# A two-layer trunk on one core: the first MLP's first half in four parts of K, and another order of instructions

## The chip, the cores and the metric

The program runs on one core of one Trainium2 chip. The metric is the device time of one execution in microseconds (us). A core has TensorE (PE, matrix products, with its weight loads shown apart as PEld), VectorE (DVE), ScalarE (ACT), GpSimd (POOL) and SyncE (SP), which in this kernel issues nearly all DMA transfers. Each engine runs its own instructions in the order in which the program lists them, and semaphores hold an instruction back until its inputs are there and its output's buffer is free. So the time depends on two things: how much each engine has to do, and in which order each engine's list puts it.

## The reference

The computation is a decoder trunk of two layers on 256 tokens of width 2048, in float32. Each layer has a mixer and an MLP, and each of the four is preceded by a modulated RMS norm and followed by a gated residual:

```python
def ada_modulate(x, c, w, b):
    mod = jax.nn.silu(c) @ w + b
    shift, scale, gate = jnp.split(mod, 3, axis=-1)
    h = rms_norm(x) * (1.0 + scale[:, None, :]) + shift[:, None, :]
    return h, gate[:, None, :]

def sq_relu_mlp(h, w1, w2):
    return jnp.square(jax.nn.relu(h @ w1)) @ w2

for layer in range(DEPTH):                      # DEPTH = 2
    h, gate = ada_modulate(x, c, ada_w[layer, 0], ada_b[layer, 0])
    y = mlstm_mixer(h, ...) if layer % 2 == 0 else rglru_mixer(h, ...)
    x = x + gate * y
    h, gate = ada_modulate(x, c, ada_w[layer, 1], ada_b[layer, 1])
    x = x + gate * sq_relu_mlp(h, mlp_w1[layer], mlp_w2[layer])
return rms_norm(x) * final_g
```

Layer 0's mixer (mLSTM) has a projection to q, k, v, o and two gates, then eight heads with two chunks of 128 tokens each, then a product with `a_w_out`. Layer 1's mixer (RG-LRU) has a projection, a convolution over time, block-diagonal gates and a scan. The MLPs are 2048 to 8192 to 2048. The four `ada_w` matrices, 2048 x 6144 each, multiply one vector `c`.

## The kernel before

**Numbers.** Everything stays transposed: features on the 128 partitions, the 256 tokens on the free axis. A float32 product is made of products of two rounded halves. `split` (L167) makes a high part `whi` on ACT (L174) and a low part `wlo` on DVE (L175) of each half of a weight tile; `pair` (L179) does so for activations (ACT L187 or L184, DVE L188 or L185). A product takes high times high, high times low and low times high. `mm2` (L198) does it in two matmuls, one of 512 columns (L200, both halves of the activation) and one of 256 (L201), and leaves two sums side by side that `halves` (L256) adds with an ACT copy (L260) and a DVE addition (L261). `mm3` (L192) does it in three matmuls of 256 columns (L194 to L196) into one sum. `mmu` (L215) is the form for activations that are not normed yet: `unnormed` (L319) has the scale and the shift in it, and `scaled` (L247) multiplies the result by the norm later, so that the products need not wait for the norm.

**Weights.** Each weight tile is 128 x 2048, 1 MB, and comes in through SP's queue (L161, `raw`) into one of four buffers. After it is split, its halves stand in four buffers for `whi` and four for `wlo`, two tiles' worth.

**Adaptive weights.** The `ada_w` matrices come as 192 tiles of 128 x 2050 (`adaraw`, L125); each costs one DVE instruction (L127) that multiplies it by `c` and adds up the rows. They are spread over the program: `pace(phase, calls)` reads from the table `PACE` how many of the 192 are to be done by the end of a phase, and each `fill()` in the phase issues its share. `need` issues one at once if it is wanted and not there. Outside the first projection these tiles use the same four buffers as the weight tiles.

**Stages.** The projection of layer 0 runs in five groups of K (`GROUPS`, `group` L487): the sums of a group go to SBUF by ACT (L537), and the next group puts them back into PSUM by ACT (L526) ahead of its products. Then come the gates, and the eight heads: `scores` (`sp`, `kp`, `E`, `qw`), `state` (`cp`, `Cn`), `head` (`num`, `den`, `hsq`) and `meansq` (`hss`). Eight weight blocks of the o projection (`ogate` L703, the accumulators from `mm_2710` on) are placed between the steps of the heads by the table `OB`. `normed` makes `zhi` and `zlo`, and the product with `a_w_out` follows: four blocks together from `awoa` (`mm_3675` to `mm_3678`), then twelve from `awo`, each ending in `residual` (L332), which adds to `xall` and squares for the norm. Then layer 0's MLP: its first 4096 hidden columns come from 32 tiles of `w1a`, in two halves of K (`kh`); the first half leaves sums in `part`, the second adds them (L421, L423). The other half of the hidden columns, the second product, layer 1's mixer (`mix1`, L773) and its MLP follow with `block` (L203).

**Order.** The kernel is written as one sequence; the tile framework reserves buffers, sets semaphores and lists each engine's instructions, in program order unless a priority moves them (L173, L126). PSUM has five banks for the products (`ps`, tiles `mm`) and three for other results (`aux`).

Of the kernel before, what the change touches and what calls it, by code (L numbers as in the profile page):

```python
# [8 lines left out]
F32 = mybir.dt.float32  # L9
F32R = mybir.dt.float32r  # L10
AF = mybir.ActivationFunctionType
# [42 lines left out]

QKV_RATE = (1.6, 0.9, 0.9, 0.9, 1)
AHEAD = 2
PACE = dict(o=51, out0=66, w1a=82, w1b=90, mlp0=162, mix1=169, out1=176, mlp1=192)


@with_exitstack  # L60
def trunk_kernel(ctx, tc, xT_d, par_d, ada_d, wqkv_d, wg_d, wo_d, awoa_d, awo_d, bwi_d, bg_d, bwo_d,
# [77 lines left out]
    def pace(phase, calls):  # L139

        pacing[:] = [max(0.0, (PACE[phase] - len(done)) / calls), 0.0]

# [21 lines left out]
    def weights(src):  # L164
        return split(load(src))
# [81 lines left out]
    def scaled(acc, r, out=None):  # L247

        if out is None:
            out = tmp.tile([P, S], F32, name="hsum", tag="t")  # L250
        V.tensor_tensor(out=out, in0=acc[:, 0:S], in1=r, op=ALU.mult)
        c = tmp.tile([P, 1], F32, name="shc", bufs=4)
        V.tensor_scalar(out=c, in0=acc[:, S:S + 1], scalar1=acc[:, S + 1:UX], scalar2=None, op0=ALU.add)
        return out, c
# [52 lines left out]
    def modulated(i, j, r, direct=False):  # L307
        need(i, 16 + j)
        need(i, j)
        t = tmp.tile([P, S], F32, name="hmod", tag="t")  # L310
        V.scalar_tensor_tensor(out=t, in0=xT[j], scalar=mod[i][:, 16 + j:17 + j], in1=r,  # L311
                               op0=ALU.mult, op1=ALU.mult)
        if not direct:
            return pair(t, bias=mod[i][:, j:j + 1])
        h = act.tile([P, 2, S], F32, name="hdirect", tag="act")[:, 0, :]
        A.activation(h, t, AF.Identity, bias=mod[i][:, j:j + 1])
        return h, pair(h)
# [14 lines left out]
    def residual(i, j, acc, norm, us=None, width=KC):  # L332

        need(i, 32 + j)
        for a in range(0, acc.shape[1], S):
            V.scalar_tensor_tensor(out=xT[j], in0=acc[:, a:a + S], scalar=mod[i][:, 32 + j:33 + j],  # L336
                                   in1=xT[j], op0=ALU.mult, op1=ALU.add)
        if norm is not None:
            norm.add(j)
        if us is not None and j < width:  # L340
            us.append(unnormed(i + 1, j))

    def finish(srcs, hid, norm):
# [30 lines left out]
                (nc.sync if i % 8 else nc.scalar).dma_start(out=out_d[:, i:i + 4, ts], in_=x4)  # L374


    def square_relu(h, c, pool):
        A.activation(h, h, AF.Relu, bias=c)  # L378
        A.activation(h, h, AF.Square)
        return pair(h, "more" if pool else "act", pool)  # L380
# [5 lines left out]
    def mlp_in(l, i, norm, us, more):  # L386
        out, us2 = Norm(), []
        hs = []
        pace("mlp1", 32)
        for q in range(FFQ):  # L390
            hid = []
            if l == 0 and q == 0:
                part = []
                for kh in range(2):
                    pace("w1b" if kh else "w1a", 16)
                    if kh == 1:
                        hs += [modulated(i, j, r) for j in range(KC // 2, KC)]
                    for jp in range(16):
                        w = weights(w1a_d[kh, jp])
                        early = kh == 0 and jp < EARLY  # L400
                        if kh == 0:
                            part.append(act.tile([P, 2, S], F32, name="part", tag="act"))
                        for jj in range(2):
                            acc = ps.tile([P, UX if early else 2 * S], F32, name="mm")
                            for kk in range(8):
                                hi, lo = w[kk // 4]
                                o = (kk % 4) * 256 + jj * P
                                (mmu if early else mm2)(acc, hi[:, o:o + P], lo[:, o:o + P],
                                                        us[kk] if early else hs[kh * 8 + kk], kk == 0, kk == 7)
                            if early:  # L410
                                if jp + jj == 0:
                                    r = norm.rstd_now()
                                _, c = scaled(acc, r, part[jp][:, jj, :])
                                A.activation(part[jp][:, jj, :], part[jp][:, jj, :], AF.Identity, bias=c)
                                if jp + jj == 0:
                                    hs += [modulated(i, j, r) for j in range(KC // 2)]
                            elif kh == 0:
                                halves(acc, part[jp][:, jj, :])
                            else:
                                h = tmp.tile([P, S], F32, name="hsum", tag="t")  # L420
                                V.tensor_tensor(out=h, in0=acc[:, 0:S], in1=part[jp][:, jj, :],  # L421
                                                op=ALU.add)
                                V.tensor_tensor(out=h, in0=acc[:, S:2 * S], in1=h, op=ALU.add)  # L423
                                hid.append(square_relu(h, 0.0, more if len(hid) >= 32 - MLP_BUFS else None))
                        fill()
                pace("mlp0", 96)
            else:
                for j in range(32):
                    if l == 1 and q == 0 and j < MORE_MLP:
                        if j == 0:  # L430
                            accs, r = quad([w1b_d[kg] for kg in range(4)], us, norm)
                        if j == 3:
                            hs += [modulated(i, j, r) for j in range(KC)]
                        t, c = scaled(accs[j] if j < 4 else early_block(w1_d[l, j], us), r)
                        hid.append(square_relu(t, c, None))
                    else:
                        hid.append(square_relu(halves(block([w1_d[l, q * 32 + j]], hs)), 0.0,
                                               more if j >= 32 - MLP_BUFS else None))
                    fill()
            for j in range(KC):  # L440
                last = q == FFQ - 1
                if last and l == 1 and j == KC - 1:
                    finish([w2_d[l, 2 * q, j], w2_d[l, 2 * q + 1, j]], hid, out)
                    break
                acc = block([w2_d[l, 2 * q, j], w2_d[l, 2 * q + 1, j]], hid,
                            mm3 if j == KC - 1 else mm2)
                residual(i, j, acc, out if last else None, us2 if last and l == 0 else None)
                fill(2)
        return out, us2
# [108 lines left out]
    with ExitStack() as mctx:  # L558
# [205 lines left out]
                        kg + kk == 6)  # L764
        for j in range(KC):
            acc = accs[j] if j < 4 else block([awo_d[j]], zs, mm3)
            residual(0, j, acc, norm, us, KC // 2)
            fill()

    norm, us = mlp(0, 1, norm, us)  # L770
# [190 lines left out]
```

## Time and profile before

| quantity | value |
|---|---|
| median of 3 runs | 2244.34 us (2240.72 to 2247.15) |
| the profiled execution's own time | 2244.5 us |
| its span in the profile | 2242.8 us |
| mean granted TensorE clock | 0.989 |
| HBM traffic | 596.93 MB read, 267 GB/s over the span |

The span leaves out 1.7 us around the program. In the views below, "busy" is the time in which an engine's records cover the clock, "idle before, releaser" is time ahead of an instruction in which its engine had nothing to do, put down to what ended it, and PEclk is the clock that TensorE was granted as a share of full speed. A slice of 40 in the page is 56 us long. Matmuls overlap in the records (a row's mean of 280 ns is not its pitch), so a rate is read from how many start in a stretch.

### The profile page before, as it was taken

The page shows a single profiled execution, that of the slowest core. Times are in us where ns is not written, and L with a number is a line of the kernel's source. Part 1 is how long each engine was busy: PE and PEld are TensorE (multiplying, and loading weights), DVE is VectorE, ACT ScalarE, POOL GpSimd, SP SyncE. Part 2 cuts the span into 40 slices and gives each one's busy share as a digit, 9 for nine tenths or more (in the row PEclk, how much of TensorE's full clock was granted, in tenths as well). Part 3 has the DMA queues.
Part 4 walks back from the last instruction along what each step waited for, and adds up shares of the span by engine and source line. Part 5 has one row for each costly group of instructions (what it writes and reads, how often), then busy time and mean ns, then how long its engine had stood idle before and what let it go on. Part 6 is the DMA issues. An engine that isn't in the chain of part 4 may idle for free.

```text
span 2242.8 us, 34191 instructions
## 1 busy us (share of the span) xinstructions
PE 2181.7 (97%) x13606; PEld 1960.5 (87%) x13606; DVE 1722.3 (77%) x2199; ACT 1286.1 (57%) x1997; POOL 90.1 (4%) x70
## 2 busy tenths in 40 slices
PE   7899899899999999999999999999999999999998
PEld 6798799788888889888889999889888889888887
DVE  6777888988898788888889988998875555555554
ACT  6677777345674335665445877756664334665443
POOL 0000010220000000000110000020000000000110
PEclk9999999899999999999999999999999999999999
DMA  8888887897788999998997665776875555555552
GB/s 345 348 325 319 307 300 255 303 337 270 285 284 319 337 322 332 328 334 319 322 335 276 211 229 208 269 276 238 307 284 203 188 188 188 188 188 188 189 188 93
DMA packets 88671, 601.25 MB, mean 268 GB/s; under 512 B 10424, under 2 KB 14648, under 8 KB 16192
## 3 DMA queue, kind: packets, MB, share of 16 engines
q1 hardware_dynamic: 86400, 598.03, 74.3%
q8 instruction: 106, 1.74, 0.3%
q10 hardware_dynamic: 2112, 1.05, 0.2%
q14 instruction: 53, 0.43, 0.1%
HBM read 596.93 MB, written 2.11 MB: 267 GB/s over the span
## 4 chain that ended last, share of the span: by engine, by line
PE 86%; DVE 7%; ACT 3%; issue 2%; DMA 1%; SPq 0%; DVEq 0%; ACTq 0%
PE mm L200 42%; PE mm L201 22%; PE mm L511 8%; DVE wlo L175 3%; PE mm L196 2%; PE mm L195 2%; PE mm L194 2%; DVE adaraw L127 2%; ACT whi L174 1%; PE mm L218 1%; PE mm L217 1%; PE mm L219 1%; DMA adaraw<-in_ada 1%; PE mm L357 0%; DVE hmod L311 0%
## 5 line engine op out<-in xcount | busy, mean ns | idle before, releaser
L200 PE MATMUL mm<-pair,whi 128*128 128x512 f32 x4272 | 1496.3, 394 | 5.0 <-DVE pair L188 3.2
L201 PE MATMUL mm<-pair,wlo 128*128 128x256 f32 x4272 | 1195.9, 280 | 0.8 <-DVE wlo L175 0.8
L175 DVE TENSOR_TENSOR wlo<-raw,whi 128x1024 fp32r<-128x1024 f32 x736 | 900.2, 1233 | 380.1 <-ACT whi L174 375.9
L174 ACT ACTIVATE whi<-raw 128x1024 fp32r<-128x1024 f32 x736 | 771.9, 1057 | 609.7 <-PE mm L200 476.7
L200 PEld LDWEIGHTS mm<-pair,whi 128*128 128x128 f32 x4272 | 802.6, 188 | 190.7 <-DVE pair L188 4.7
L201 PEld LDWEIGHTS mm<-pair,wlo 128*128 128x128 f32 x4272 | 804.7, 188 | 1.7 <-DVE wlo L175 1.1
L127 DVE SCALAR_TENSOR_TENSOR adaraw<-adaraw,cbc 128x2050 f32<-128x2050 f32 x192 | 439.7, 2291 | 50.7 <-DMA adaraw<-in_ada 41.7
L511 PE MATMUL mm<-pair,whi 128*128 128x256 f32 x736 | 136.0, 288 | 10.7 <-ACT pair L187 5.7
L511 PEld LDWEIGHTS mm<-pair,whi 128*128 128x128 f32 x736 | 115.8, 194 | 12.9 <-ACT pair L187 6.3
L194 PE MATMUL mm<-pair,whi 128*128 128x256 f32 x432 | 123.1, 285 | 0.0
L195 PE MATMUL mm<-pair,whi 128*128 128x256 f32 x432 | 122.0, 282 | 0.0
L196 PE MATMUL mm<-pair,wlo 128*128 128x256 f32 x432 | 121.4, 281 | 0.0
L511 PE MATMUL mm<-pair,wlo 128*128 128x256 f32 x368 | 104.0, 288 | 2.9 <-DVE wlo L175 2.9
L336 DVE SCALAR_TENSOR_TENSOR xall<-mm,mod,xall 128x256 f32<-128x256 f32 x170 | 81.0, 480 | 27.0 <-PE mm L201 18.7
L378 ACT ACTIVATE hsum<-hsum 128x256 f32<-128x256 f32 x121 | 49.2, 413 | 81.7 <-DVE hsum L261 71.3
L291 POOL TENSOR_TENSOR nacc<-nacc,nsq 128x256 f32<-128x256 f32 x52 | 75.6, 1453 | 351.0 <-ACT nsq L282 350.7
L196 PE MATMUL mm<-zhi,wlo 128*128 128x256 f32 x256 | 75.8, 296 | 6.6 <-DVE wlo L175 6.6
L194 PEld LDWEIGHTS mm<-pair,whi 128*128 128x128 f32 x432 | 81.9, 190 | 0.4
L194 PE MATMUL mm<-zhi,whi 128*128 128x256 f32 x256 | 74.9, 297 | 7.6 <-ACT zhi L731 5.5
L195 PEld LDWEIGHTS mm<-pair,whi 128*128 128x128 f32 x432 | 81.8, 189 | 0.0
L196 PEld LDWEIGHTS mm<-pair,wlo 128*128 128x128 f32 x432 | 81.8, 189 | 0.0
L511 PE MATMUL mm<-whi,pair 128*128 128x512 f32 x256 | 81.0, 394 | 0.0
(218 smaller groups left out, 2054.7 us busy)
## 6 DMA issues: line engine op xcount, KB each, us to landing
raw<-in_w SPq DMA_DIRECT2D x220, 1024.0 KB, 5.1
adaraw<-in_ada SPq DMA_DIRECT2D x192, 1025.0 KB, 6.6
raw<-in_wqkv SPq DMA_DIRECT2D x40, 1024.0 KB, 8.5
raw<-in_w1a SPq DMA_DIRECT2D x32, 1024.0 KB, 6.2
raw<-in_bwi SPq DMA_DIRECT2D x28, 1024.0 KB, 5.0
raw<-in_bwo SPq DMA_DIRECT2D x16, 1024.0 KB, 5.1
raw<-in_awo SPq DMA_DIRECT2D x12, 1024.0 KB, 5.5
raw<-in_wo SPq DMA_DIRECT2D x8, 1024.0 KB, 6.2
```

Of the source, the lines that this page charges most:

```text
L127: V.scalar_tensor_tensor(out=raw, in0=raw, scalar=1.0, in1=cbc, op0=ALU.mult, op1=ALU.mult, accum_out=mod[i][:, j:j + 1])
L174: A.activation(hi, sl, AF.Copy)
L175: V.tensor_tensor(out=lo, in0=sl, in1=hi.bitcast(F32), op=ALU.subtract)
L194: PE.matmul(out, lhsT=whi, rhs=hi, start=first, stop=False)
L195: PE.matmul(out, lhsT=whi, rhs=lo, start=False, stop=False)
L196: PE.matmul(out, lhsT=wlo, rhs=hi, start=False, stop=last)
L200: PE.matmul(out, lhsT=whi, rhs=p.rearrange("p a t -> p (a t)"), start=first, stop=False)
L201: PE.matmul(out[:, 0:S], lhsT=wlo, rhs=p[:, 0, :], start=False, stop=last)
L291: G.tensor_tensor(out=self.acc, in0=self.acc, in1=sq, op=ALU.add)
L336: V.scalar_tensor_tensor(out=xT[j], in0=acc[:, a:a + S], scalar=mod[i][:, 32 + j:33 + j], in1=xT[j], op0=ALU.mult, op1=ALU.add)
L378: A.activation(h, h, AF.Relu, bias=c)
L511: PE.matmul(out, lhsT=l, rhs=m, start=clear and kk + n == 0, stop=kk == gn - 1 and n == len(ops) - 1, skip_group_check=True)
```

## The change

Three things change. The first half of layer 0's first MLP product runs in four parts of K (`kg`) instead of two, with eight tiles of 512 columns each. Two blocks of 128 columns share a PSUM bank. `go_on` makes three matmuls of 256 columns per product as `mm3` does. From the second part on, ACT copies the sums from `part` back into PSUM ahead of the products; after the first three parts ACT copies them out; after the fourth, ACT applies relu to 512 columns at a time, DVE squares, and `pair` splits. `early_part` does the first two tiles on activations that are not normed yet, four at a time, so `residual` now makes four of these (after blocks 8, 10, 12 and 14) instead of eight (after blocks 0 to 7). The weights are laid out for this on the host.

The table `PACE` now asks for 58 adaptive tiles by the end of the product with `a_w_out` instead of 66, and for 66, 74, 82 and 84 by the ends of the four parts instead of 82 and 90 by the ends of the two halves. What it asks for at the end of the MLP and later is the same.

The tile framework is told to order the instructions by its own simulated time line. That applies to the whole program.

```diff
-PACE = dict(o=51, out0=66, w1a=82, w1b=90, mlp0=162, mix1=169, out1=176, mlp1=192)
+PACE = dict(o=51, out0=58, w1_0=66, w1_1=74, w1_2=82, w1_3=84, mlp0=162, mix1=169, out1=176, mlp1=192)
...
-        if us is not None and j < width:
+        if us is not None and width == 4:
+            if j >= KC // 2 and j % 2 == 0:
+                us.append(unnormed(i + 1, j // 2 - 4))
+        elif us is not None:
             us.append(unnormed(i + 1, j))
...
+    def go_on(out, whi, wlo, p, clear, last):
+        ops = ((whi, p[:, 0, :]), (whi, p[:, 1, :]), (wlo, p[:, 0, :]))
+        for n, (lhsT, rhs) in enumerate(ops):
+            PE.matmul(out, lhsT=lhsT, rhs=rhs, start=clear and n == 0, stop=last and n == 2,
+                      skip_group_check=True)
+
+    def early_part(w, us, norm, part):
+        accs = []
+        for b in range(4):
+            acc = ps.tile([P, UX], F32, name="mm")
+            for kk in range(4):
+                hi, lo = w[kk // 2]
+                o = kk % 2 * 512 + b * P
+                mmu(acc, hi[:, o:o + P], lo[:, o:o + P], us[kk], kk == 0, kk == 3)
+            accs.append(acc)
+        if norm is not None:
+            norm.now = norm.rstd_now()
+            norms[:] = [norm.now]
+        for b, acc in enumerate(accs):
+            t = part[b // 2][:, b % 2, :]
+            _, c = scaled(acc, norms[0], t)
+            A.activation(t, t, AF.Identity, bias=c)
...
+                for kg in range(4):
+                    pace(f"w1_{kg}", 6)
+                    for c in range(8):
+                        if kg == 0 and c == 1:
+                            hs += [modulated(i, j, r) for j in range(4)]
+                        w = weights(w1a_d[kg, c])
...
+                            for b2 in range(2):
+                                acc = ps.tile([P, 2, S], F32, name="mm")
+                                sums = part[2 * c + b2]
+                                if kg > 0:
+                                    A.activation(acc, sums, AF.Copy)
+                                for jj in range(2):
+                                    for kk in range(4):
+                                        hi, lo = w[kk // 2]
+                                        o = kk % 2 * 512 + (2 * b2 + jj) * P
+                                        go_on(acc[:, jj, :], hi[:, o:o + P], lo[:, o:o + P], hs[4 * kg + kk],
+                                              kg + jj + kk == 0, kk == 3)
+                                if kg < 3:
+                                    A.activation(sums, acc, AF.Copy)
+                                    continue
+                                A.activation(sums, acc, AF.Relu)
+                                V.tensor_tensor(out=sums, in0=sums, in1=sums, op=ALU.mult)
+                                for jj in range(2):
+                                    own = len(hid) < 32 - MLP_BUFS
+                                    hid.append(pair(sums[:, jj, :], "act" if own else "more", None if own else more))
+                        if c < 6:
+                            fill()
+                        elif c == 6 and kg < 3:
+                            hs += [modulated(i, j, r) for j in range(4 * kg + 4, 4 * kg + 8)]
...
-            residual(0, j, acc, norm, us, KC // 2)
+            residual(0, j, acc, norm, us, 4)
...
-    with tile.TileContext(nc) as tc:
+    with tile.TileContext(nc, schedule_with_timeline_sim=True) as tc:
```

Three places show how the order moves. The first is PE's list between head 0 and head 1 of the mLSTM, before: the end of head 0 (`den`), the next head's scores (`sp`, `kp`), and the first of the `mm_2908` matmuls, a block of the o projection.

```order
L676 MATMUL den_2866<-E_2780,ones_85 128x128
L677 MATMUL den_2866<-qw_2785,Cn_2794 128x128
L639 MATMUL sp_2882<-qk0_187,qk4_191 128x128 x2
L194 MATMUL mm_2908<-pair_220,whi_2911 128x256
L641 MATMUL kp_2885<-ident_87,qk4_191 128x128
L195 MATMUL mm_2908<-pair_220,whi_2911 128x256
L196 MATMUL mm_2908<-pair_220,wlo_2912 128x256
L194 MATMUL mm_2908<-pair_233,whi_2911 128x256
```

In all, 21 matmuls of `mm_2908` stand between `kp` and `hss` there, and 26 more between `cp` and `num`. The same place in the changed program, from the end of head 0 to head 1's `num`:

```order
L708 MATMUL num_2859<-qw_2785,Cn_2794 128x128
L712 MATMUL den_2866<-qw_2785,Cn_2794 128x128
L674 MATMUL sp_2882<-qk0_187,qk4_191 128x128 x2
L676 MATMUL kp_2885<-ident_87,qk4_191 128x128
L728 MATMUL hss_2899<-hsq_2877,ones_85 128x256
L729 MATMUL hss_2899<-hsq_2877,ones_85 128x256
L696 MATMUL cp_2903<-v0_195,kw_2887 128x256
L697 MATMUL cp_2903<-ones_85,kw_2887 128x128
L706 MATMUL num_2972<-E_2889,v0_195 128x128
L707 MATMUL num_2972<-E_2889,v1_196 128x128
```

The o blocks have moved: seven of the eight now stand ahead of head 0's `cp`, 166 matmuls of them between `kp` and `cp` of head 0, and the last, `mm_3522`, is spread over the steps of heads 1 and 2. Later heads have pieces of `mm_3675` to `mm_3678` between their steps.

The second place is SP's list of DMA issues around the start of the product with `a_w_out`, before (rows of the same kind are counted, as x6):

```order
L161 DMA raw<-in_awoa 128x2048 x2
L634 DMA MB<-rows_d 128x512
L125 DMA adaraw<-in_ada 128x2050 x6
L161 DMA raw<-in_awo 128x2048
L125 DMA adaraw<-in_ada 128x2050 x2
L161 DMA raw<-in_awo 128x2048
L125 DMA adaraw<-in_ada 128x2050 x2
L161 DMA raw<-in_awo 128x2048
L125 DMA adaraw<-in_ada 128x2050 x2
L161 DMA raw<-in_awo 128x2048
```

and after:

```order
L161 DMA raw<-in_awoa 128x2048
L669 DMA MB<-rows_d 128x512
L125 DMA adaraw<-in_ada 128x2050
L669 DMA MB<-rows_d 128x512
L125 DMA adaraw<-in_ada 128x2050
L161 DMA raw<-in_awo 128x2048
L669 DMA MB<-rows_d 128x512
L161 DMA raw<-in_awo 128x2048
L669 DMA MB<-rows_d 128x512 x2
L125 DMA adaraw<-in_ada 128x2050
L161 DMA raw<-in_awo 128x2048 x2
```

Between the last `awoa` tile and the last `awo` tile, 22 adaptive tiles are issued before and 7 after; the others come in the MLP.

The third place is ACT's list at the end of layer 1's mixer, after: `th`, `aa`, `TT` and `gb` belong to the last blocks of the recurrence, and `whi_14723` is the second half of the fourth of the weight tiles (`bwo`) of the product that follows.

```order
L184 ACTIVATE pair_14537<-gb_14114 128x256
L874 ACTIVATE aa_13951<-th_14383,sp4_11954 128x256
L876 ACTIVATE TT_13949<-th_14383,sp2_11932 128x256
L871 ACTIVATE th_14394<-gacc_14387,hbra_11956 128x256
L897 ACT_TABLE_LOAD
L897 ACTIVATE gb_14398<-gb_14398 128x512
L895 ACT_TABLE_LOAD
L895 ACTIVATE TT_13949<-TT_13949 128x512
L174 ACTIVATE whi_14723<-raw_14717 128x1024
```

and before, where the same recurrence ends:

```order
L839 ACTIVATE aa_13563<-th_13995,sp4_11566 128x256
L174 ACTIVATE whi_14226<-raw_14220 128x1024
L841 ACTIVATE TT_13561<-th_13995,sp2_11544 128x256
L855 ACTIVATE gb_14010<-mm_14011 128x256
L855 ACTIVATE gb_14010<-mm_14071 128x256
L860 ACT_TABLE_LOAD
L860 ACTIVATE TT_13561<-TT_13561 128x512
L174 ACTIVATE whi_14278<-raw_14276 128x1024
L862 ACT_TABLE_LOAD
```

Before, weight halves stand between the steps of the recurrence; after, none stands between `pair_14537` and `TT_13949`.

More of the change, by code (lines that the diff above doesn't have):

```diff
@@ L374, in finish @@
                 (nc.sync if i % 8 else nc.scalar).dma_start(out=out_d[:, i:i + 4, ts], in_=x4)
+    def go_on(out, whi, wlo, p, clear, last):
[19 more added lines that the diff above has]
+            A.activation(t, t, AF.Identity, bias=c)
+    norms = []
     def square_relu(h, c, pool):
@@ L393, in mlp_in @@
                 part = []
[L394 to L425, printed above, removed]
@@ new lines, in mlp_in @@
+                for kg in range(4):
[4 more added lines that the diff above has]
+                        w = weights(w1a_d[kg, c])
+                        if kg == 0:
+                            part += [act.tile([P, 2, S], F32, name="part", tag="act") for _ in range(2)]
+                        if kg == 0 and c < EARLY:
+                            early_part(w, us, norm if c == 0 else None, part[2 * c:])
+                            if c == 0:
+                                r = norm.now
+                        else:
+                            for b2 in range(2):
[21 more added lines that the diff above has]
+                            hs += [modulated(i, j, r) for j in range(4 * kg + 4, 4 * kg + 8)]
@@ L940 @@
         "bwo": cols(a["b_w_out"][0]),
-        "w1a": a["mlp_w1"][0][:, 0:2 * DM].reshape(2, 8, P, 16, 256).transpose(0, 3, 2, 1, 4).reshape(2, 16, P, DM),
+        "w1a": a["mlp_w1"][0][:, 0:2 * DM].reshape(4, 4, P, 8, 512).transpose(0, 3, 2, 1, 4).reshape(4, 8, P, DM),
         "w1b": quads(a["mlp_w1"][1][:, 0:512]),
```

## The prediction

> **What bounds the kernel now.** I read the page's busy shares and the chain first, then the windows of 50 us, then TensorE's waits.
>
> ```profile
> span 2242.8 us, 34191 instructions
> PE 2181.7 (97%) x13606; PEld 1960.5 (87%) x13606; DVE 1722.3 (77%) x2199; ACT 1286.1 (57%) x1997; POOL 90.1 (4%) x70
> PE 86%; DVE 7%; ACT 3%; issue 2%; DMA 1%; SPq 0%; DVEq 0%; ACTq 0%
> ```
>
> PE is busy for 2181.7 of 2242.8 us, so 61 us of idle time, and what the clock loses, are all that an order can win back. The windows show where they lie (columns: busy time and count of PE, PEld, DVE, ACT, POOL, then PE's granted clock, DMA share, GB/s).
>
> ```profile
> 50.00:100.00 50.00, 43.06 (x288) 40.11 (x287) 37.80 (x39) 32.69 (x50) 0.00 (x0) 0.93 0.87 337
> 100.00:150.00 50.00, 50.00 (x357) 46.74 (x357) 39.77 (x42) 38.58 (x57) 0.00 (x0) 1.00 0.85 324
> 150.00:200.00 50.00, 48.25 (x311) 43.10 (x310) 38.86 (x39) 35.69 (x54) 0.00 (x0) 1.00 0.91 345
> 200.00:250.00 50.00, 46.37 (x272) 40.02 (x272) 38.29 (x36) 32.40 (x48) 0.00 (x0) 0.97 0.78 297
> 250.00:300.00 50.00, 42.97 (x280) 39.48 (x280) 40.30 (x57) 40.20 (x72) 1.33 (x2) 0.94 0.82 295
> 300.00:350.00 50.00, 50.00 (x403) 48.96 (x402) 42.73 (x57) 37.78 (x73) 6.11 (x4) 0.99 0.81 297
> ...
> 500.00:550.00 50.00, 47.34 (x270) 40.71 (x269) 46.17 (x70) 27.44 (x44) 0.00 (x0) 1.00 0.74 266
> 550.00:600.00 50.00, 49.73 (x284) 43.16 (x283) 41.27 (x59) 27.68 (x47) 0.00 (x0) 1.00 0.81 290
> 600.00:1200.00 600.00, 600.00 (x3474) 526.95 (x3473) 513.12 (x606) 312.42 (x475) 18.90 (x13) 1.00 0.90 322
> 1200.00:1600.00 400.00, 398.40 (x2763) 368.72 (x2762) 360.58 (x592) 283.32 (x458) 19.42 (x15) 1.00 0.69 245
> 1600.00:2200.00 600.00, 600.00 (x3473) 527.20 (x3472) 339.67 (x387) 306.31 (x441) 14.11 (x12) 1.00 0.59 203
> ```
>
> From 600 to 2200 us PE loses 1.6 us in all. There a new order can only lose. What can be won lies before 550 us: in the projection (75 to 298), and in the end of the heads and the product with `a_w_out` (out0, 390 to 510). The heads between, at 300 to 350, are covered: 50.00 of 50. Windows of 10 us show out0:
>
> ```profile
> 380.00:390.00 10.00, 10.00 (x75) 9.40 (x73) 10.00 (x11) 4.47 (x10) 0.00 (x0) 1.00 0.95 346
> 390.00:400.00 10.00, 4.40 (x35) 4.07 (x34) 10.00 (x13) 3.98 (x4) 0.00 (x0) 1.00 0.99 357
> 400.00:410.00 10.00, 6.91 (x30) 6.61 (x31) 7.36 (x10) 2.33 (x4) 0.00 (x0) 0.52 0.92 327
> ...
> 430.00:440.00 10.00, 5.94 (x33) 5.74 (x32) 10.00 (x12) 4.29 (x7) 3.87 (x2) 0.73 0.87 307
> ...
> 470.00:480.00 10.00, 7.21 (x46) 6.80 (x45) 8.28 (x9) 4.22 (x5) 0.72 (x1) 0.83 0.86 309
> ```
>
> Where PE stops, DVE is at 10.00 of 10 and the DMA share is near 1: the adaptive tiles fill both. TensorE's waits name the parts:
>
> ```profile
> PE mm L196 <- DVE wlo L175: 6.6, 3, 4.1
> PE mm L511 <- ACT pair L187: 5.7, 2, 4.7
> PE mm L194 <- ACT zhi L731: 5.5, 1, 5.5
> PE mm L511 <- ACT mm L526: 4.8, 1, 4.8
> ...
> PE mm L200 <- DVE pair L188: 3.2, 4, 2.0
> PE cp L661 <- ACT kw L643: 2.2, 1, 2.2
> ```
>
> **The change part by part.** The sum is made against the profiled execution, 2244.5 us (span 2242.8 and 1.7 around it), which is the median of the runs to 0.2. The prices:
>
> ```profile
> L175 DVE TENSOR_TENSOR wlo<-raw,whi 128x1024 fp32r<-128x1024 f32 x736 | 900.2, 1233 | 380.1 <-ACT whi L174 375.9
> L174 ACT ACTIVATE whi<-raw 128x1024 fp32r<-128x1024 f32 x736 | 771.9, 1057 | 609.7 <-PE mm L200 476.7
> L127 DVE SCALAR_TENSOR_TENSOR adaraw<-adaraw,cbc 128x2050 f32<-128x2050 f32 x192 | 439.7, 2291 | 50.7 <-DMA adaraw<-in_ada 41.7
> L526 ACT ACTIVATE mm<-v 128x512 f32<-128x512 f32 x32 | 19.1, 600 | 0.6
> L664 ACT ACTIVATE Cn<-cp 128x384 f32<-128x384 f32 x8 | 3.9, 488 | 7.2 <-PE cp L662 7.2
> L688 ACT ACTIVATE hsq<-num 128x512 f32<-128x512 f32 x8 | 4.8, 602 | 0.0
> ```
>
> **Out0.** The slots ahead of the last `awo` tile hold 7 adaptive tiles instead of 22: 15 x 2.29 = 34 us of DVE and 15 MB go to the MLP, where DVE has room (513 of 600 us). The four stretches above lost 5.6, 6.4 (10 less 6.91 x 0.52), 5.7 and 4.0 us, in all 21.7. The end of the heads is also a chain of its own (norm, `zhi`, `zlo`), so not all of it goes: at least 6 of the 9.7 us of the last two, which have no chain of their own, should go; at most all 21.7. I take **-15**, nearer to the full loss since DVE is the bound in each row. Late next is that chain.
>
> **Projection, 75 to 298.** The 4.8 us wait for the seed copy, 1.75 us at 150, 3.6 at 200 and some 3 of clock (0.03 x 50 and part of the 0.06 x 50) come from instructions that stand one or two places after what they wait for. In the new order those places have more work between. Between nothing and 13 us; I take **-10**.
>
> **The step from group 0 to group 1.** The 4.7 us wait for `pair` at 65 to 70 us is a wait for the adaptive tiles that modulate four K rows. In the new order two `wlo` halves (2 x 1.23) stand on DVE ahead of `pair_513`, and SP issues two weight tiles more ahead of the adaptive ones: 2.5 us at least, and one more transfer (1 MB at 337 GB/s is 3.1 us, an estimate) at most 6. I take **+4**.
>
> **Heads.** The o blocks leave the heads. At four of the seven boundaries between heads (into 1, 2, 4 and 6) `kp`, `hss` and `cp` now stand one behind the other or with less than a dozen matmuls between their inputs and them. The nearest row is the 2.2 us wait of `cp` for `kw`, behind six o matmuls of 0.7 us: 2.9 us from `kp` to `cp`, against which a bare boundary has only `hss`, 0.8 us (two of about 0.4). So 2.1 a boundary, 8.4 for four; then `Cn` (0.49) and `hsq` (0.60) come bare at the same places, some 2 more. What hid all this was 284 o matmuls, and they now run in a stretch where nothing waits. Bounds: nothing, if the quad's pieces cover it as the o blocks did at 300 to 350; 16, if every boundary (7 x 2.2) pays. I take **+10**.
>
> **The MLP's first half.** 480 products take three matmuls of 256 columns instead of one of 512 and one of 256. Their pitch:
>
> ```profile
> 443.00:463.00 20.00, 20.00 (x172) 20.00 (x171) 18.77 (x17) 8.97 (x13) 7.63 (x4) 1.00 0.94 348
> 700.00:800.00 100.00, 100.00 (x573) 87.40 (x572) 78.90 (x79) 38.24 (x36) 0.00 (x0) 1.00 0.91 322
> ```
>
> 172 in 20 us of `mm3` are 349 ns for three; 573 in 100 us of `mm2` are 349 ns for two. The edges of the first window are worth a matmul each, 4 ns a product, 0 to 2 us; I take 1. ACT gets 48 seeds, 44 copies out and 16 relus of 0.60 us, 65 us, and loses some 36 of smaller ones; a tile of 48 matmuls (5.6 us) then has about 4.5 us of ACT work. The nearest rows are the projection's, which seeds and empties banks in the same way: it lost nothing at 100 to 150, 1.75 at 150 and 3.6 at 200, 5.4 us in 150, so 6.6 in the 185 us of these tiles, 13 at the worst window's rate, 0 at the best. I take 6. The wait for the norm (2.7 at 500 to 550, 0.3 after) is replaced by one as long: four unnormed products are its cover. Together **+7**, -2 to +14. The adaptive tiles that come here (26 instead of 16) cost DVE 23 us, and the halves and sums that go give some 27 back.
>
> **End of layer 1's mixer.** Between `pair_14537` and `whi_14723` ACT now has six pieces of the recurrence and two table loads:
>
> ```profile
> L836 ACT ACTIVATE th<-gacc,hbra 128x256 f32<-128x256 f32 x32 | 13.2, 464 | 7.2 <-PE gacc L196 7.1
> L860 ACT ACT_TABLE_LOAD x8 | 10.3, 1283 | 0.1
> ...
> L839 ACT ACTIVATE aa<-th,sp 128x256 f32<-128x256 f32 x16 | 9.6, 600 | 0.1
> L841 ACT ACTIVATE TT<-th,sp 128x256 f32<-128x256 f32 x16 | 9.5, 592 | 0.0
> ...
> L862 ACT ACTIVATE gb<-gb 128x512 f32<-128x512 f32 x8 | 5.1, 633 | 0.1
> ```
>
> 0.60 + 0.59 + 0.46 + 2 x 1.28 + 2 x 0.63 + 1.06 for the half itself = 6.5 us; PE has three to six products of 349 ns, 1 to 2 us, as cover: 4.5 late. A `wlo` behind five residual additions a little later adds about 1.5. The window 1200 to 1600 lost 1.6 us before. I take **+6**, 0 (if ACT runs that far ahead) to 9.
>
> A granted clock below 1 follows idle time: 0.52 at 400 to 410 after the 5.5 us wait for `zhi`, and 0.83 at 470 to 480 with 2.8 us idle. [...]
>
> Sum: -15 - 10 + 4 + 10 + 7 + 6 = **+2**, so 2246.5 us. All lower ends give -34, all upper ends +39.
>
> **The rivals.**
>
> - *The heads and the MLP stay covered.* If the pieces of the quad hide the heads as the o blocks did, and ACT keeps ahead in the MLP and the mixer, the terms of +10, +7 and +6 become 0, +1 and 2: 2244.5 - 15 - 10 + 4 + 0 + 1 + 2 = 2226. For it: PE lost nothing at 300 to 350 with DVE at 42.73 and ACT at 37.78 of 50, so neither is near its limit there. Against it: the cover is gone from four boundaries.
> - *Bare heads lose the clock* (slower). Each wait of 2 us is followed by a stretch at a lower clock, as at 470 to 480, where a loss of 2.8 us idle came with 0.17 of 7.21 us, 1.2, and at 430 to 440, where 4.1 came with 1.6. At eight heads with 2.2 + 1.5 us each the term is 30 instead of 10: 2266. It decides from the point at which the waits at more than five boundaries reach 2 us.
> - *Out0 is bound by transfers, not by DVE*, and the change does not do there what it could: shares of 0.95 to 0.99 at 380 to 400 speak for it. Then only 6 of the 15 us come: 2255.5. Against it: the 15 MB leave the same queue.
>
> **How the numbers follow.** The forecast's own case, in which gains and new waits nearly cancel (2233 to 2259), gets 0.44; covered heads 0.30; the clock 0.18; transfers 0.08. A measurement of this kernel can tell 0.3%, 6.7 us, from no change: faster is under 2237.6, slower over 2251. The forecast's case gives 0.10 faster, 0.24 same, 0.10 slower; the first rival 0.30 faster; the second 0.18 slower; the third 0.03 same and 0.05 slower: **0.40, 0.27, 0.33**. The range takes in both rivals, reaches 10 us below the first for the lower ends of out0 and the projection, and 4 above the second: **2216 to 2270**. What lies beyond, toward 2211 and 2283 where every term is at its end, I give 1 in 6. The forecast case's own is 2233 to 2259.
>
> **What would show it.** In the changed profile: DVE below 10.00 in the 10 us windows of out0 and no wait for `zhi` above 2 us there (out0); no wait for L526's successor above 2 us between 100 and 290 (projection); waits of `cp` and `hss` for `kw` and `hsq`, some 2 us each at heads 1, 2, 4 and 6 (heads); PE busy for 97% of the first MLP's tiles (MLP); one wait of 4 to 5 us for `whi` at the end of layer 1's mixer. The prediction is wrong if PE's wait in the heads is under 4 or over 20 us, or if a wait appears after 1600 us, where the lists are the same.

## The result and the profile after

The change makes the kernel slower: 2297.2 us (median of 4 runs, 2290.96 to 2304.26) against 2245.7 (4 runs), ratio 1.0228, 95% interval 1.0202 to 1.0254. The prediction was 2246.5 us with a range to 2270, so it was wrong, in size and in sense. Four executions took far longer (3059 us in e1, 3813 in e8 and 2405 in h2 below, and 7391 of the kernel before); the ratios and intervals leave them out, and the medians given, which are over all runs, would move by under 3 us without them. The page of the changed kernel:

```profile
span 2296.6 us, 35051 instructions
...
PE 2199.0 (96%) x14086; PEld 1993.7 (87%) x14086; DVE 1696.8 (74%) x2123; ACT 1318.2 (57%) x2012; POOL 75.2 (3%) x70
...
PE 77%; DMA 8%; DVE 7%; ACT 6%; issue 2%; SPq 0%; DVEq 0%; ACTq 0%
```

PE's share of the chain falls from 86 to 77%, and DMA's rises from 1 to 8%. The windows of 50 us (columns as before) show where:

```profile
50.00:100.00 50.00, 36.94 (x257) 35.31 (x256) 41.56 (x45) 26.44 (x42) 0.00 (x0) 0.83 0.82 301
...
200.00:250.00 50.00, 50.00 (x320) 45.06 (x320) 37.13 (x33) 37.98 (x53) 0.00 (x0) 1.00 0.82 313
...
300.00:350.00 50.00, 43.47 (x336) 41.63 (x335) 34.60 (x47) 28.55 (x56) 2.20 (x5) 0.96 0.83 301
350.00:400.00 50.00, 36.87 (x230) 33.32 (x231) 29.61 (x48) 31.14 (x64) 2.10 (x3) 0.84 0.28 98
400.00:450.00 50.00, 43.70 (x342) 43.23 (x341) 32.50 (x44) 23.62 (x39) 7.68 (x7) 0.92 0.43 149
...
500.00:550.00 50.00, 43.14 (x340) 42.45 (x341) 40.11 (x63) 30.25 (x48) 0.00 (x0) 0.93 0.77 275
...
1250.00:1300.00 50.00, 46.74 (x336) 44.45 (x335) 42.09 (x79) 30.57 (x46) 0.00 (x0) 0.93 0.57 207
1300.00:1350.00 50.00, 44.82 (x311) 41.51 (x310) 36.03 (x66) 38.56 (x61) 0.00 (x0) 0.97 0.50 176
...
1450.00:1500.00 50.00, 41.58 (x223) 33.83 (x222) 41.82 (x73) 33.28 (x56) 4.27 (x3) 0.97 0.58 211
...
1600.00:1650.00 50.00, 46.73 (x254) 40.20 (x255) 41.34 (x65) 32.65 (x61) 0.00 (x0) 0.97 0.76 269
```

The projection is better (three full windows from 100 us on, of which one is shown), and so is the product with `a_w_out`; the start, the heads (325 to 412) and most of 1250 to 1500 and 1600 to 1650 are worse. The DMA share of 0.28 at 350 to 400 says that few transfers ran there either. TensorE's waits:

```profile
PE mm L194 <- ACT zhi L766: 14.7, 4, 6.3
PE mm L546 <- ACT pair L187: 10.4, 2, 7.1
...
PE mm L217 <- DVE shc L253: 5.9, 1, 5.9
...
PE kp L676 <- ACT ad L715: 4.9, 3, 2.3
PE cp L696 <- ACT kw L678: 4.1, 3, 2.2
PE mm L194 <- ACT gb L890: 3.9, 4, 1.7
...
PE gacc L194 <- ACT pair L184: 2.8, 3, 1.3
```

The table adds up, for each stretch, its length less PE's busy time times the granted clock, from windows of 5 us ("lost"). The stretches end at the first `gp` (gates), the last `hss` (heads), the norm of the first MLP, 205 us later (its first half), the first and the last `gacc` (mixer), the norm of the second MLP, 90 us later, and the end.

| stretch | before | after | difference | predicted |
|---|---|---|---|---|
| 0 to 80 us, start | 23.7 | 29.7 | +6.0 | +4 |
| projection, to the gates | 12.8 | 4.3 | -8.5 | -10 |
| gates and heads | 3.5 | 27.1 | +23.6 | +10 |
| out0 | 23.9 | 8.3 | -15.6 | -15 |
| first MLP's first half | 2.9 | 13.6 | +10.7 | +7 |
| rest of the first MLP | 0.2 | 0.7 | +0.5 | 0 |
| layer 1's mixer | 1.1 | 20.0 | +18.9 | together +6 |
| its product, and 90 us of the second MLP | 0.3 | 11.7 | +11.4 | |
| the rest | 9.8 | 9.5 | -0.3 | 0 |
| sum | 78.2 | 124.9 | +46.7 | +2 |

The span grew by 53.8 us; the 7.1 that the table lacks are time that it does not count as lost (more in the last section).

### The profile page after: what moved, and what is told of

Its sections match the earlier page's. It is cut to its first block, busy times and chain, and to the rows that moved or that the text cites. A ratio compares the mean times of both kernels' runs of the same rounds, so it can differ in the third digit from the quotient of the medians.

```text
span 2296.6 us, 35051 instructions
## 1 busy us (share of the span) xinstructions
PE 2199.0 (96%) x14086; PEld 1993.7 (87%) x14086; DVE 1696.8 (74%) x2123; ACT 1318.2 (57%) x2012; POOL 75.2 (3%) x70
## 4 chain that ended last, share of the span: by engine, by line
PE 77%; DMA 8%; DVE 7%; ACT 6%; issue 2%; SPq 0%; DVEq 0%; ACTq 0%
PE mm L200 33%; PE mm L201 17%; PE mm L546 10%; PE mm L385 6%; DMA adaraw<-in_ada 6%; DVE adaraw L127 2%; PE mm L195 2%; PE mm L194 2%; PE mm L196 2%; DVE wlo L175 2%; ACT whi L174 1%; PE mm L218 1%; PE mm L217 1%; PE mm L219 1%; DMA raw<-in_bwi 1%
## 5 line engine op out<-in xcount | busy, mean ns | idle before, releaser
L200 PE MATMUL mm<-pair,whi 128*128 128x512 f32 x3792 | 1334.4, 395 | 9.3 <-DVE pair L188 5.0
L175 DVE TENSOR_TENSOR wlo<-raw,whi 128x1024 fp32r<-128x1024 f32 x736 | 894.9, 1228 | 402.6 <-ACT whi L174 399.4
L200 PEld LDWEIGHTS mm<-pair,whi 128*128 128x128 f32 x3792 | 714.5, 189 | 176.7 <-DVE pair L188 6.2
L127 DVE SCALAR_TENSOR_TENSOR adaraw<-adaraw,cbc 128x2050 f32<-128x2050 f32 x192 | 439.7, 2293 | 73.0 <-DMA adaraw<-in_ada 63.1
L385 PE MATMUL mm<-pair,whi 128*128 128x256 f32 x960 | 171.8, 283 | 2.9 <-ACT whi L174 1.8
L385 PEld LDWEIGHTS mm<-pair,whi 128*128 128x128 f32 x960 | 147.3, 190 | 4.0 <-ACT whi L174 2.5
L546 PE MATMUL mm<-pair,whi 128*128 128x256 f32 x736 | 134.1, 286 | 13.0 <-ACT pair L187 10.4
L546 PEld LDWEIGHTS mm<-pair,whi 128*128 128x128 f32 x736 | 114.9, 193 | 14.9 <-ACT pair L187 10.9
L194 PE MATMUL mm<-pair,whi 128*128 128x256 f32 x432 | 121.9, 282 | 3.9 <-ACT gb L890 3.9
L195 PE MATMUL mm<-pair,whi 128*128 128x256 f32 x432 | 121.2, 281 | 0.0
L194 PEld LDWEIGHTS mm<-pair,whi 128*128 128x128 f32 x432 | 81.3, 188 | 5.1 <-ACT gb L890 4.7
L217 PE MATMUL mm<-unnormed,whi 128*128 128x258 f32 x272 | 78.3, 289 | 5.9 <-DVE shc L253 5.9
```

The costliest lines, as they stand in the source:

```text
L127: V.scalar_tensor_tensor(out=raw, in0=raw, scalar=1.0, in1=cbc, op0=ALU.mult, op1=ALU.mult, accum_out=mod[i][:, j:j + 1])
L175: V.tensor_tensor(out=lo, in0=sl, in1=hi.bitcast(F32), op=ALU.subtract)
L194: PE.matmul(out, lhsT=whi, rhs=hi, start=first, stop=False)
L195: PE.matmul(out, lhsT=whi, rhs=lo, start=False, stop=False)
L200: PE.matmul(out, lhsT=whi, rhs=p.rearrange("p a t -> p (a t)"), start=first, stop=False)
L217: PE.matmul(out[:, 0:UX], lhsT=whi, rhs=u[:, 0:UX], start=first, stop=False)
```

## The experiments

### The order and the rest apart

```diff
 e1 (the changed kernel)
-    with tile.TileContext(nc, schedule_with_timeline_sim=True) as tc:
+    with tile.TileContext(nc) as tc:
 e2 (the kernel before)
-    with tile.TileContext(nc) as tc:
+    with tile.TileContext(nc, schedule_with_timeline_sim=True) as tc:
 e3 (the kernel before)
-PACE = dict(o=51, out0=66, w1a=82, w1b=90, ...)
+PACE = dict(o=51, out0=58, w1a=74, w1b=84, ...)
```

> The changed kernel in all but the order: the four-part MLP and the new table of adaptive tiles, with the instructions listed as in the kernel before. Theory A (the simulated time line's order costs the time, some 50 us, and the rest of the change gains or is neutral): 2228 to 2245 us, with out0's waits shrunk by 10 to 15 us. Theory B (the four-part MLP costs it, by its copies on ACT and its 480 more matmuls): 2280 us or more. If both share it, 2260.

> The kernel before with nothing changed but the order by the simulated time line. Theory A: 2280 to 2310 us, with the losses of the changed kernel in the heads (some 25 us) and in layer 1's mixer and product (some 25 us). Theory B: 2235 to 2250 us.

> The kernel before with 58 adaptive tiles instead of 66 by the end of out0, and 74 and 84 by the ends of the MLP's halves instead of 82 and 90. If out0 gains because DVE gets fewer adaptive tiles: 2230 to 2236 us, and TensorE's waits for zhi and wlo at 390 to 480 us shrink from 12 us to under 4. If out0's gain in the changed kernel came from the order: 2242 to 2248 us with the waits as before.

Measured: e1 2250.1 us, ratio 1.002 (1.0007 to 1.0032); e2 2310.8, 1.028 (1.0255 to 1.0305); e3 2249.3, 1.0016 (1.0004 to 1.0029). Theory A holds in this: the order alone costs 65 us on the old code, just over the expected range (40.2 us lost in gates and heads, 32.4 in the mixer, its product and the 90 us behind; some 25 each were expected), and some 47 on the new (2297.2 less 2250.1). The rest of the change is worth nothing: e1 missed the expected 2228 to 2245. e3 lies above both of its ranges. e1's windows in out0 are free of loss, as this one:

```profile
430.00:440.00 10.00, 10.00 (x87) 10.00 (x86) 6.68 (x7) 4.70 (x6) 1.50 (x2) 1.00 0.88 314
```

Out0 lost 0.3 us instead of 23.9. But the first MLP gave it back: 14.3 us lost in its first half instead of 2.9, and 8.5 in its rest instead of 0.2. TensorE's waits of e1, first at 455 to 500, then from 500 to 1240 us:

```profile
PE mm L217 <- DVE shc L253: 5.6, 1, 5.6
PE mm L385 <- DVE pair L188: 2.0, 1, 2.0
```

```profile
PE mm L201 <- DVE wlo L175: 8.4, 9, 1.5
```

The first two are the wait for the norm and for the modulated activations behind it, 10.7 us lost from 465 to 490 us with the clock. The third is a wait for DVE, which now has the adaptive tiles that out0 no longer does: it spends 19.1 us on them in out0 instead of 43.4, and from 500 to 1240 us 222 instead of 202. e3 shows that the table of adaptive tiles alone does not free out0: it lost 18.0 us there (23.9 before), and DVE still spent 31.6 us on adaptive tiles there. The eight `unnormed` of the old code call for their adaptive tiles in out0 whatever the table says; that four of them, made late, are what lets the table work is the likeliest reading, but no run changes them alone.

### One engine's list in the heads or the mixer

These keep the instructions that one engine has in a stretch in written order by dependencies without a wait, and leave the rest to the simulated time line. The helper, and its calls:

```diff
+    def pin(start, engines):
+        last = {}
+        for ins in nc.cur_bb.bb.instructions[start:]:
+            e = str(ins.engine)
...
+            if e in last:
+                tc.add_manual_dep(ins, last[e].name, mybir.DependencyInfo(mybir.DependencyClass.NoSync, ...), reason="pin")
+            last[e] = ins
 e4, from the heads on; e5 and e6 from the gates on:
+        pin(begun, ("PE",))             # e4
+        pin(begun, ("PE", "SP"))        # e5
+        pin(begun, ("SP",))             # e6
 e7 and e8, layer 1's mixer:
+        pin(begun, ("PE",))                 # e7
+        pin(begun, ("PE", "Activation"))    # e8, but for split's
```

> The changed kernel with TensorE's instructions of the eight heads and the o projection kept in the order in which the kernel is written (the o blocks between the steps of the heads); all else is ordered by the simulated time line. Theory A1 (the heads lose because their cover stands ahead of them): the loss of 26 us there falls under 8, 2272 to 2282 us. Rival A2 (they lose by ACT's table loads and by SP's list, in which MB waits stand ahead of weight tiles): 2290 us or more.

> The changed kernel with SP's and TensorE's instructions from the gates to the end of the heads kept in written order (so the small transfers rows_d, mlast and MB no longer stand behind weight and adaptive tiles that wait for buffers); ACT and DVE by the simulated time line. Theory C (the heads lose because these transfers come late, so that head 0 starts 27 us late and the o blocks are spent before it): cp of head 0 at 300 to 308 us instead of 325, the loss from the gates to the end of the heads under 10 us instead of 27, 2270 to 2280 us. Rival D (ACT's and DVE's lists hold the heads up: table loads, adaptive tiles ahead of the gates' chain on DVE): cp not before 315 us, 2288 us or more.

> As the run before it, but with only SP in written order; TensorE by the simulated time line. Theory C: most of the gain comes with SP alone, 2272 to 2285 us. If the late transfers and the moved o blocks need each other: over 2288 us.

> The changed kernel with TensorE's instructions of layer 1's mixer in written order; all else by the simulated time line. Theory A' (the mixer loses because its small products run bare): its loss of 20 us falls under 8, 2278 to 2287 us. Rival (ACT's list: 18 table loads and the recurrence ahead of the copies that free PSUM and of the weight halves): 2292 us or more.

> As the run before it, and ACT's instructions of layer 1's mixer too, but for the weights' high halves, in written order. If ACT's list is the cause: the mixer's loss falls under 6 us and that of the product behind it (7 us) under 2, 2272 to 2282 us. If neither list is: 2290 us or more.

Measured: e4 2294.0 us, e5 2307.2, e6 2309.0, e7 2339.1, e8 2367.3. The theories that one or two lists do it all fall; the times lie in or beyond the ranges of their rivals. In the mixer a second list makes it worse than one (e8 against e7). In e4 PE loses 10.8 us from head 0's first `cp` to the last `hss` instead of 25.4, but from the gates to that `cp` 18.9 instead of 1.8: the wait has moved ahead of the heads (TensorE's waits of e4):

```profile
PE cp L711 <- ACT kw L693: 18.1, 1, 18.1
...
PE gp L671 <- DVE g L659: 7.6, 1, 7.6
```

PE now comes to head 0's `cp` 18.1 us before `kw` is there. In the changed kernel the o blocks were run in that time, so it did not show as a wait. So the chain that head 0 needs is itself late. The chain that ended last, before (start, duration, what):

```profile
284.93 1.47 DMA rows_d<-rows
...
287.68 7.39 DMA MB<-rows_d
...
298.14 1.22 PE cp L661 x2
```

The gates' rows are written at 284.93, and `cp` starts at 298.14. SP's issues in the changed kernel (start, duration, what):

```profile
303.75 0.35 SPq L650 DMA_DIRECT2D rows_d<-rows  x1
305.75 0.35 SPq L125 DMA_DIRECT2D adaraw<-in_ada  x1
308.72 0.33 SPq L161 DMA_DIRECT2D raw<-in_wo  x1
310.93 0.33 SPq L125 DMA_DIRECT2D adaraw<-in_ada  x1
311.35 0.44 SPq L652 DMA_DIRECT2D mlast<-rows_d  x1
```

and its chain behind them:

```profile
311.84 10.72 DMA MB<-rows_d
...
325.61 1.12 PE cp L696 x2
```

The rows are issued 19 us later than before, the read of `mlast` only 7.6 us behind them because two adaptive tiles and a weight tile stand between on SP's list, and the transfer of `MB` takes 10.72 us instead of 7.39; `cp` starts 27 us later. The 19 us arise on DVE. ACT hands the gates to DVE no later (DVE's first step of this chain, into `ls`, starts at 263.40 us, 264.51 before); then DVE's list puts 14 `wlo` halves (L175) and 6 adaptive tiles (L127) between the steps of the chain, where the kernel before has 4 and 3. A piece of DVE's list, before and then after (start, duration, what):

```profile
267.05 0.41 DVE L588 TENSOR_TENSOR ls<-lse 8x256 f32<-8x256 f32 x1
...
267.70 2.27 DVE L127 SCALAR_TENSOR_TENSOR adaraw<-adaraw,cbc 128x2050 f32<-128x2050 f32 x1
...
269.91 2.64 DVE L591 SCALAR_TENSOR_TENSOR ls<-ls 8x256 f32<-8x256 f32 x6
```

```profile
270.69 1.21 DVE L175 TENSOR_TENSOR wlo<-raw,whi 128x1024 fp32r<-128x1024 f32 x1
271.83 0.28 DVE L624 TENSOR_SCALAR ls<-ls 8x256 f32<-8x256 f32 x1
272.04 2.27 DVE L127 SCALAR_TENSOR_TENSOR adaraw<-adaraw,cbc 128x2050 f32<-128x2050 f32 x1
...
274.25 1.21 DVE L175 TENSOR_TENSOR wlo<-raw,whi 128x1024 fp32r<-128x1024 f32 x1
```

That SP's list is the cause (theory C) is not settled by e5 and e6. In both the gates themselves moved, to 265 and 267 us from 299: PE waits 12.9 us for `g` and 11.9 for a `whi`, and though e6 has head 0's `cp` at 298.2, as early as before, it loses 30.9 us in gates and heads. An early `cp` alone is thus not enough. The run h2 below, with all lists but SP's put back, speaks against theory C.

In e7 one list put back is worse than none, by 42 us:

```profile
PE gacc L211 <- ACT pair L201: 46.1, 13, 10.8
```

PE's written order asks for the pairs of the recurrence where ACT's and DVE's simulated lists do not have them yet.

### All lists of a stretch

The next runs take, for a stretch, the order in which e1's program has its instructions on each engine, written into the kernel as lists of instruction numbers, and add the same dependencies along them:

```diff
+    def as_listed(start):
+        here = {i.name: i for i in nc.cur_bb.bb.instructions[start:]}
+        for listed in LISTED:
...
+                i = here.get(f"I-{n}")
...
+                    tc.add_manual_dep(i, last.name, mybir.DependencyInfo(mybir.DependencyClass.NoSync, ...), reason="listed")
 f1 (gates to the end of out0):
+    as_listed(begun)
     norm, us = mlp(0, 1, norm, us)
 f2 (layer 1's mixer and its product):
+    as_listed(begun)
     mlp(1, 3, norm, us)
 f3: f1 and f2; f4: f3 and the start to the end of group 1
```

> The changed kernel, in which from the gates to the end of out0 the instructions of all five engines stand to one another as in e1 (the same code in written order); the rest by the simulated time line. Theory E (the lists of the engines fit one another: a stretch loses its stalls when all of them are put back together, where one engine's list alone, e4 to e6, moved or raised them): the loss from the gates to the end of out0 falls from 35 to under 6 us, 2262 to 2272 us. Rival F (the stretch is late because of what the simulated order did ahead of it): over 2285 us.

> The same for layer 1's mixer and the product behind it. Theory E: the loss of 20 and 7 us there falls to under 4 in all, 2264 to 2274 us. Rival F: over 2285 us, as when TensorE alone was put back (2339 us).

> Both stretches. Theory E: the gains add up, 2232 to 2244 us. If the second only moves what the first gains: 2255 us or more.

> Both stretches and the start up to the end of group 1. Theory E: 6 us less than the run before it, 2226 to 2238 us, which is faster than the kernel before: what is left of the simulated order then covers the rest of the projection, where it gained 8 us, and the first MLP. Otherwise 2240 us or more.

Measured: f1 2268.1 us (ratio 1.0098, 1.0071 to 1.0125), f2 2269.8 (1.0101, 1.0079 to 1.0123), f3 2243.4 (0.9987, 0.9974 to 0.9999), f4 2246.4 (0.9993, 0.998 to 1.0007). Theory E holds, and the gains add up: 29.1 and 27.4 us apart, 53.8 together. In f1 what is left of TensorE's waits from 283 to 470 us is:

```profile
PE kp L703 <- ACT ad L742: 2.0, 1, 2.0
PE cp L723 <- ACT kw L705: 1.4, 1, 1.4
```

The stretches' losses fall from 27.1 and 8.3 to 3.4 and 0.2 (f1), and from 20.0 and 7.0 to 1.3 and 0.2 (f2). The start won 5.4 us back (f4: 24.3 lost), but the projection behind it lost 6.8 more (15.0 against 8.2), so f4 is no faster than f3; its forecast of 2226 to 2238 was a miss. None of these versions is clearly faster than the kernel before: f3's interval ends just under 1.

### Which lists, and the norm

```diff
 h1: f1 without TensorE's list; h2: f1 without SP's; m1: f2 without TensorE's
 g1: f3, and in early_part
+            if norm is None and b in (1, 2):
+                acc = aux.tile([P, UX], F32, name="mm", tag="aux")
+            else:
+                acc = ps.tile([P, UX], F32, name="mm")
```

> As f1, from the gates to the end of out0, but TensorE's list is left to the simulated time line (o blocks ahead of the heads). Theory G (the heads lose because the gates' chain on ACT, DVE and SP is late; what TensorE's list does matters little): 2264 to 2274 us. Rival H (the bare heads of the prediction: once the chain is on time TensorE's list costs 10 us or more): 2278 us or more.

> As f1, but SP's list is left to the simulated time line (the small transfers stand behind tiles that wait for buffers). If SP's list holds the chain up: 2280 us or more. If ACT's and DVE's lists do: 2264 to 2274 us.

> As f2, layer 1's mixer and the product behind it, but TensorE's list is left to the simulated time line. If ACT's and DVE's lists are the cause there: 2266 to 2276 us. If TensorE's list is as much: 2283 us or more, with its waits for gacc's and gb's copies as in the changed kernel.

> As f3, with two of the four sums of the second early tile of the first MLP in banks of the pool aux, so that TensorE has 12 to 16 more products to do before it needs the norm (4 to 5 us). If the wait of 5.8 us for the norm is one for PSUM banks: it falls under 2 us, and the time to 2234 to 2240 us, under that of the kernel before. If not: 2241 to 2247 us, as f3.

Measured: h1 2286.2 us (ratio 1.0186, 1.0169 to 1.0203), h2 2270.7 (1.0116, 1.0099 to 1.0133), m1 2303.2 (1.0263, 1.0247 to 1.0279), g1 2246.2 (1.0016, 1.0004 to 1.0028). With the gates' chain on time (head 0's `cp` at 298.7 us), TensorE's list still costs 18 us (2286.2 less f1's 2268.1); in the table's terms 9.3 of them are lost in gates and heads (12.7 against 3.4), 5.4 in out0 (5.6 against 0.2), and the rest mostly in the mixer, which neither run touches (22.8 against 18.1). Rival H holds there; its waits from 283 to 485 us in h1:

```profile
PE mm L219 <- ACT whi L199: 3.6, 2, 2.6
PE mm L219 <- ACT zhi L792: 3.2, 1, 3.2
PE hss L754 <- ACT hsq L749: 2.5, 2, 2.2
PE mm L221 <- DVE wlo L200: 2.5, 3, 1.4
```

They are bare steps: `hss` for `hsq`, of which the prediction spoke, the blocks for their halves, the quad for `zhi`. The other lists are worth 11 us in time (2297.2 to 2286.2), and 17.1 of the stretch's own losses (14.4 in gates and heads, 2.7 in out0), of which the projection and the mixer give back 3.8 and 2.8. h2, which leaves SP's list to the simulated time line, has an interval that overlaps f1's, so SP's is not needed; that leaves ACT's, DVE's and POOL's. For the late chain the trace names DVE's; ACT's and DVE's were not tried apart. In the mixer the two cannot be parted: without TensorE's list nothing is won (m1), without the others more is lost (e7).

g1 is a miss. TensorE's waits at 460 to 500 us, f3 and then g1:

```profile
PE mm L243 <- DVE shc L279: 5.8, 1, 5.8
```

```profile
PE mm L411 <- DVE shc L279: 4.5, 1, 4.5
PE mm L243 <- DVE shc L279: 2.1, 1, 2.1
```

More banks only move the wait for `shc` to the products behind, and it grows from 5.8 to 6.6 us: what is late is DVE's work on the first sums after the norm.

## Why the prediction was wrong

**The projection (-10) and out0 (-15)** came out at -8.5 and -15.6. The projection's gain is the order's, as the step had it: e1, in written order, still loses 11.2 us there (12.8 before, 4.3 in the changed kernel). In out0 e1 and e3 show the reason: fewer adaptive tiles on DVE, and not the order. e1, without the simulated order, won 23.6 there: a little over the upper end (21.7) that the prediction worked out and discounted. That the changed kernel came out at -15.6 is in part luck: its out0 has lost 8.3 us to the order, which the -15 did not price. The third rival (transfers) falls.

**The start (+4)** measured +6.0, the upper end of its bounds, with the wait for `pair` at 7.1 us.

**Heads (+10, bounds 0 to 16)** is the first step that failed: gates and heads lost 23.6 us more. The step has the heads grow longer at bare boundaries and takes it that head 0 starts when it did before. But from head 0's first `cp` to the last `hss` the changed kernel needs 86.6 us, the kernel before 88.8. What changed is the start, 27.5 us later, and the cover: 29.8 us more of PE's work stands ahead of that `cp`, and 25.8 less beside the heads. The sign that was named, waits of `cp` and `hss`, hardly shows: 4.1 us, of which 2.2 are head 0's, and 0.2. The quad's pieces, which the first rival counted as cover, wait themselves for `zhi` (8.4 us between 345 and 412 us). The mechanism of the step is there once the chain is on time: in h1 the heads take 98.6 us, and gates and heads lose 9.3 more than in f1, close to the +10. What the prediction put at nothing is the rest, 14.4 us: it read TensorE's list and not the gates' chain on DVE ahead of it, which came 19 us late, so that the o blocks were spent in waiting for it.

**End of layer 1's mixer (+6)** is the second and larger one: 30 us. The prediction saw the right risk ("There a new order can only lose") and then priced one place, `whi` behind the recurrence. TensorE's waits show no wait like that one (the longest for `whi` there is 1.4 us, where 4.5 were expected); they are for `gb`, `pair`, `wlo` and `whi`, up to 3.3 us each, all through the mixer, its product and the second MLP's first tiles. A stretch that lost 1.6 us in 400 has cover everywhere; a new order can open any piece of it. f2 shows that it goes when all lists do, but for 5.6 us in the second MLP, where f2 leaves the order as it was; which list opens it stays open. (The list in the prediction shows five pieces of the recurrence, not six; the sum counts five.)

**"A wait after 1600 us, where the lists are the same"** was itself an error: the simulated order reaches through the second MLP's first tiles, and 4.7 us are lost there (0.2 before, 1.0 in e1).

**The MLP's first half (+7)** lost 10.7 more, and it is not the order's: e1 loses 11.4 more there. Nor is it shown to be the four parts': e3, with the old code and only the new table, loses 11.1 us there (2.9 before), though at other waits. No wait names ACT's copies, the 6 us of the term: TensorE's waits there are for `shc` (5.9), which the prediction put at no change, and 4.1 for halves and pairs (the halves on ACT 1.8). The count of adaptive tiles was off too: the old table puts 24 in this half (90 less 66), not 16, and DVE's time on them rose from 44.6 to 57.4 us, not by 23. The pitch was right: `go_on`'s triples start every 0.353 us (654.80 to 661.86 us, 20 of them), 4 ns above the pairs of `mm2`, 2 us in all.

**The lost clock (second rival)** is part of it. Between 325 and 412 us PE was idle for 18.1 us and lost 25.6; the 7.5 between are the clock. It was not what decided.

## What to carry to other kernels

A change of the order is priced on every stretch that it touches, and most of all on those that lose nothing, since there only new waits can come; reading the places that lose time finds the gains and misses the losses. The lists of the engines fit one another: a stretch was put back here with all of its lists (in the heads SP's was not needed), and one list pinned alone against the others can cost more than the fault (42 us here). A chain of small steps on one engine is read on that engine's list: each large instruction that the order puts between two steps delays all that waits at the chain's end (here ten `wlo` halves of 1.21 us and three adaptive tiles of 2.27 us more than before, 18.9 us together, ahead of rows that were issued 19 us later). Work moved off an engine in one stage is worth what it frees there less what it fills elsewhere: out0 gained 23.6 us, and the MLP behind it gave 19.7 back.

## What was not expected of the hardware

The granted clock fell after less idle time than in the prediction's rows, of which the one at 470 to 480 has the least, 2.8 us (waits of 2.03 and 0.76 us). The windows around head 0's `cp` in the changed kernel:

```profile
320.00:325.00 5.00, 3.43 (x30) 3.22 (x28) 4.36 (x8) 2.41 (x9) 0.83 (x2) 1.00 1.01 407
325.00:330.00 5.00, 4.39 (x22) 4.21 (x23) 2.44 (x3) 2.91 (x7) 0.00 (x0) 0.66 1.01 424
...
350.00:355.00 5.00, 1.28 (x4) 0.99 (x5) 4.84 (x9) 2.10 (x5) 0.00 (x0) 0.50 0.56 189
355.00:360.00 5.00, 5.00 (x20) 4.46 (x20) 1.00 (x2) 1.31 (x4) 0.00 (x0) 0.51 0.12 48
```

PE waited 2.18 us for `kw` up to 325.6, and the granted clock of the 5 us from 325 on is 0.66. In a longer wait (4.6 us for `zhi`, up to 353.6) and after it, it is 0.50 and 0.51 in the windows from 350 to 360.

The same instructions ran at slightly different rates. In the second MLP, where before and e1 have the same code and neither waits, 500 us held (before, then e1):

```profile
1700.00:2200.00 500.00, 500.00 (x2899) 439.62 (x2898) 267.46 (x300) 243.72 (x334) 14.11 (x12) 1.00 0.56 189
```

```profile
1700.00:2200.00 500.00, 500.00 (x2878) 437.57 (x2877) 265.52 (x298) 241.09 (x331) 13.06 (x11) 1.00 0.53 187
```

2899 matmuls against 2878, 0.7% fewer at a granted clock of 1.00; the changed kernel has 2895 there, and f3 2883. From the second MLP's first matmul (1510.3 and 1509.2 us) to the last norm (2224.0 and 2229.3) that is 6.4 us, and e1 is 5.2 slower in all. Whether this belongs to the program or to the execution was not tried. The 7.1 us that the table of losses does not hold may be of this kind, but for the 2 of the pitch: the span less the losses is 2164.6 us before and 2171.7 in the changed kernel, but 2168.0 in e3 and 2172.4 in e2, which have the old code.
